# Expert weights as chunks of 2 k-tiles by 1024 columns, gate then linear then down, with 1024-column activation and bias rows padded to 128

## The chip, the cores and the metric

The kernel runs on one core of a Trainium2 chip. The metric is the device time of one execution in microseconds, taken as the median of several runs. The engines are named as in the profile: PE (TensorE; PEld is its weight load), DVE (VectorE), ACT (ScalarE), POOL (GpSimd) and SP (SyncE, which here only issues transfers).

## The reference

The kernel computes one layer of a diffusion backbone on 512 tokens of width 1024: a windowed attention, a pooling mixer and an output projection, then 32 experts of which each token takes 4. Of this the change touches the experts:

```python
# each token: softmax over its 4 best of 32 router logits; expert e on its tokens:
gu = h2 @ w_gu[e] + b_gu[e]                 # (tokens, 2048): gate half, linear half
g = minimum(gu[:, :1024], 7.0)
l = clip(gu[:, 1024:], -7.0, 7.0)
a = (l + 1) * g * sigmoid(1.702 * g)
y = a @ w_down[e] + b_down[e]               # (tokens, 1024)
...
out = rmsnorm(x + gate2 * sum over the 4 experts of weight * y, final_g)
```

Inputs, weights and the output are float32.

## The kernel before, in words

The front part (to about 640 us) computes the attention, the mixer, the router and the tables that say which tokens go to which expert; the change leaves it alone but for two small constants. Then 32 experts follow, each with room for 96 tokens (CAP). A loop for overfull experts stands behind; it runs zero times on this input.

**Precision by splitting.** A float32 weight is used as a sum of two parts of a shorter format (F32R): `hi`, the cast, and `lo`, what the cast left over. The same is done with the tokens (`xT`, gate and linear input, transposed) and the activations (`aT`, input of the down projection). A product is three matmuls: hi x hi, lo x hi, hi x lo (activation part first).

**Chunks.** All expert weights, 32 x 12 MB, come as 384 chunks of 1 MB. A chunk is 4 k-tiles (4 x 128 rows of the weight matrix) by 512 columns, a tile of 128 x 4 x 512 and so 2 KB a row piece. Step c of the main loop does, in this order in the program: the cast of chunk c+3 on ACT (`mwh`, L1508), the operations due at this step, the subtraction of chunk c+3 on DVE (`mwl`, L1514), the load of chunk c+11 into a raw slot (`mw`, queue of SP, L1188), the remaining operations due, then the 12 matmuls of chunk c (L1250, from `mm_chunk`), of 96 x 128 by 128 x 512 each. There are 8 raw slots (RS; a different order R0 for the first seven loads), 4 hi slots (HS) and 4 lo slots (LS).

**The order of chunks.** `GU` and `DN` give it. For each expert: gate, first 512 columns (two chunks, j=0); the second half of the preceding expert's down projection; linear j=0, gate j=1, linear j=1; the first half of its own down projection. At the second chunk of each of the four pieces a bias matmul follows (L1313): `selm` picks the expert's row, `bgh` holds 32 hi rows and 32 lo rows of all biases, so it runs on 64 rows. There are 128 of them.

**Work due at fixed steps.** A table `due`, filled by `at(step, function)`, places the rest between the chunks: `f_gm` (min), `f_sgm` (sigmoid, ACT), `f_gs` (product), `f_av` (clip, then product), each on 96 x 512 and twice per expert; `f_aT` and `f_x` (4 transposes on PE, hi and lo out of PSUM on ACT and DVE, L125), `f_y` (two halves, the down result times the token's weight, DVE) with the scatter that adds y to the result rows `acc` in memory (POOL, L1254), `f_gather` (token rows for an expert two on, POOL, tile `xgb`), and for experts 2 to 9 a share of the context bias (`abps`, tables). Names beginning with `f_ab`, `f_c`, `f_s`, `f_l` belong to these.

**The tail.** The last expert's result does not go through memory: it is put out by matmuls with a one-hot table (`fin`, L1388) and added (L1389) to `fx`, the rows of `acc` loaded back after the scatter of expert 30 (L1377); a final norm and the output follow. In the tail the lo of chunk 381 is on POOL (`PLO`) and the last lo's are ordered by hand (`los`).

Of the kernel before, what the change touches and what calls it, by code (L numbers as in the profile page):

```python
# [19 lines left out]
P = 128  # L20
# [48 lines left out]
def body(ctx, tc, x, c, cx, c_ctx, w_ada, b_ada, norm1_g, norm2_g, w_in, b_in, attn_sink, w_pool,  # L69
# [1109 lines left out]
    RS, HS, LS = (9, "wa1", 4, 10, 5, 6, 3, 2), (7, 0, 1, 18), (14, 19, 16, 13)  # L1179
    R0 = (9, 10, 4, 5, 6, 3, 2)  # L1180
    mr = {"r": 0, "h": 0, "x": 0}

    def mload(src):
        r = mr["r"]
        i = R0[r] if r < len(R0) else RS[(r - len(R0)) % len(RS)]
        raw = wa([P, 4, L], F32, "mw", 1) if i == "wa1" else slot(i, [P, 4, L], F32, "mw")
        mr["r"] += 1
        nc.sync.dma_start(raw, src)  # L1188
        return raw

    def msplit(raw):
        hi = slot(HS[mr["h"] % len(HS)], [P, 4, L], F32R, "mwh")
        lo = slot(LS[mr["h"] % len(LS)], [P, 4, L], F32R, "mwl")
        mr["h"] += 1
# [47 lines left out]
    def new_aT(j):  # L1242
        return slot(("17a", "17b")[j], [P, 2, 4, CAP], F32R, f"aT{j}")
# [54 lines left out]
    def bg_load():  # L1298
        bg["r"] = slot(18, [2 * NE, 2 * D], F32, "bgr")
        for i in range(2):  # L1300
            nc.sync.dma_start(bg["r"][i * NE:(i + 1) * NE, :], b_gu)

    def bg_hi():
        bg["h"] = slot(15, [2 * NE, 2 * D], F32R, "bgh")
        act.copy(bg["h"], bg["r"])
# [11 lines left out]
    def chunk_mm(st, kind, j, kh, w):  # L1317
        if kind == "d":
            if kh == 0 and j == 0:
                st["dn"] = [ps_b(("PV", "PJ")[q], "dn")[0:CAP] for q in range(2)]  # L1320
            mm_chunk(st["dn"][j], lambda a, kk: st["aT"][kh][:, a, kk - 4 * kh, :], kh, w, kh == 0, kh == 1)
            return
        if kh == 0:
            st[kind] = ps_s("gu")[0:CAP, 0:L]
        mm_chunk(st[kind], lambda a, kk: st["xT"][:, a, kk, :], kh, w, kh == 0, False)
        if kh == 1:
            st["bias"](st[kind], (D if kind == "l" else 0) + j * L)
# [12 lines left out]
    def f_av(st):  # L1340
        ln = wb([P, L], F32, "ln")[0:CAP]
        dve.tensor_scalar(ln, st["l"], LIMIT, -LIMIT, op0=ALU.min, op1=ALU.max)
        st["av"] = wk.tile([P, L], F32, tag="tv", bufs=1, name="av")[0:CAP]
        dve.scalar_tensor_tensor(st["av"], ln, 1.0, st["gm"], op0=ALU.add, op1=ALU.mult)

    def f_aT(st, j):
        if j == 0:
            st["aT"] = [None, None]
        st["aT"][j] = new_aT(j)
        trans_split(st["av"], st["aT"][j][:, 0], st["aT"][j][:, 1])  # L1350
# [16 lines left out]
    def fin_load():  # L1367
        fin["y"] = slot(3, [P, 2, D], F32R, "yhl")
        fin["g"] = slot(2, [P, D], F32, "fgr")
        nc.sync.dma_start(fin["g"], bc_row(final_g, D))  # L1370
        fin["j"] = slot(7, [P, D], F32, "fjk")
        fin["x"] = [slot((4, 10, 5, 6)[t], [P, 2, D], F32, "fx") for t in range(NT)]
        fx_load()
# [123 lines left out]

    def do_load(c):
        if c < len(chunks):
            raws[c] = mload(chunk_src(*chunks[c]))  # L1500

    def do_hi(c):
        if c < len(chunks):
            raw = raws.pop(c)
            hi = slot(HS[mr["h"] % len(HS)], [P, 4, L], F32R, "mwh")
            lo = slot(LS[mr["h"] % len(LS)], [P, 4, L], F32R, "mwl")
            mr["h"] += 1
            act.copy(hi, raw)  # L1508
# [15 lines left out]
    base = 0  # L1524
    for e in range(NE):
        st, n = ST[e], base
        w = 2 if e else 0
        pos = lambda s_: n + s_ - (0 if s_ < 2 else 2 - w)
        nx = pos(12)
        at(pos(2 if e else 4), f_gm, st), at(pos(2 if e else 4), f_sgm, st), at(pos(3 if e else 5), f_gs, st)  # L1530
        last = e == NE - 1
        at(pos(6), f_av, st)
        if not last:
            at(pos(8), f_aT, st, 0)
        at(pos(8), f_gm, st), at(pos(8), f_sgm, st), at(pos(9), f_gs, st)
        if last:
            at(pos(8), f_aT, st, 0)
        at(pos(10), f_av, st)
        at(pos(11) if last else nx, f_aT, st, 1)
        at(nx + (1 if last else 3), f_y, st, 0), at(nx + (2 if last else 4), f_y, st, 1)  # L1540
        if not last:
            at(pos(10), f_x, ST[e + 1], 0), at(pos(11), f_x, ST[e + 1], 1)
# [197 lines left out]
```

## Time and profile before

| | before |
|---|---|
| median of 3 runs | 1895.07 us (1890.53 to 1896.86) |
| profiled execution, its own time | 1895.16 us |
| its span | 1893.3 us |
| mean granted clock | 0.971 |
| PE busy in the span | 1767.9 us (93%), 8318 matmuls |
| DVE busy | 1627.4 us (86%) |
| ACT busy | 1138.3 us (60%) |
| POOL busy | 498.8 us (26%) |

The span is the profiled execution from its first to its last instruction; 1.9 us of its time lie outside. Busy shares are averages over a front part of 640 us and the experts behind it, which have other limits, and so say little by themselves; the rows further down are taken from stretches of the experts' part. A granted clock of 1.00 is 2.4 GHz.

### The profile page before, as it was taken

The numbers are of one execution on the slowest core, as the hardware profiler recorded it, in microseconds if no ns is written. First come the engines' busy times: TensorE is split into PE (matmuls) and PEld (weight loads), VectorE is DVE, ScalarE is ACT, GpSimd is POOL, SyncE is SP. The second block draws the span as 40 slices with busy tenths as digits, with TensorE's granted clock in tenths as the row PEclk, the third lists the DMA queues.
The fourth block names the chain that finished last, engine by engine and source line by source line (L and its number), as shares of the span: only waits on it lengthen the run. The fifth ranks groups of instructions, "written<-read, shape, count | busy, mean of one in ns | idle before, by whom it ended". The sixth has DMA issues, their size and how long they took to land.

```text
span 1893.3 us, 22494 instructions
## 1 busy us (share of the span) xinstructions
PE 1767.9 (93%) x8318; PEld 1257.9 (66%) x8318; DVE 1627.4 (86%) x1791; ACT 1138.3 (60%) x1221; POOL 498.8 (26%) x288
## 2 busy tenths in 40 slices
PE   4987989999999599999999999999999999999995
PEld 2676767877679466656666666666666666666663
DVE  6479998848875689888999999999999999999995
ACT  3255657763242266656676666667667676766763
POOL 5035544322441301212121112211311221131111
PEclk8799999999999799999999999999999999999997
DMA  9032322234555589999999999999999999999983
GB/s 323 1 112 67 126 88 88 78 129 146 196 189 202 183 296 356 332 320 339 353 355 338 357 362 352 350 359 363 350 355 361 352 354 357 359 352 351 362 313 108
DMA packets 278987, 508.06 MB, mean 268 GB/s; under 512 B 12561, under 2 KB 69022, under 8 KB 278810
## 3 DMA queue, kind: packets, MB, share of 16 engines
q1 hardware_dynamic: 271242, 487.97, 73.6%
q0 software_dynamic: 7632, 18.61, 4.2%
q8 instruction: 67, 1.10, 0.2%
q14 instruction: 46, 0.38, 0.1%
HBM read 490.02 MB, written 24.79 MB: 272 GB/s over the span
## 4 chain that ended last, share of the span: by engine, by line
PE 64%; DVE 4%; DMA 1%; issue 0%; POOL 0%; ACT 0%; SPq 0%; DVEq 0%; POOLq 0%; ACTq 0%
PE gu L1250 37%; PE dn L1250 18%; PE trps L1232 3%; PE gu L1313 3%; PE ops L131 2%; DVE mwl L1514 1%; DMA xgb<-h2d,igs 1%; DMA fx<-acc 0%; PE lgps L1092 0%; DVE xh L1071 0%; DVE xh L1057 0%; PE abps L1276 0%; DVE fx L1389 0%; PE h2ps L1085 0%; DVE fx L1402 0%
## 5 line engine op out<-in xcount | busy, mean ns | idle before, releaser
L1508 ACT CAST mwh<-mw 128x2048 fp32r<-128x2048 f32 x384 | 733.1, 1911 | 346.1 <-PE gu L1250 226.0
L1514 DVE TENSOR_TENSOR mwl<-mw,mwh 128x2048 fp32r<-128x2048 f32 x381 | 867.9, 2283 | 61.9 <-ACT mwh L1508 61.7
L1250 PE MATMUL gu<-mwh,xT 128*96 128x512 f32 x2048 | 647.7, 397 | 0.0
L1250 PEld LDWEIGHTS gu<-mwh,xT 128*96 128x96 f32 x2048 | 322.7, 162 | 143.8 <-issue 14.1
L1250 PE MATMUL gu<-mwl,xT 128*96 128x512 f32 x1024 | 404.9, 395 | 0.0
L1254 POOL DMA_INDIRECT acc<-y,igs x31 | 151.1, 4874 | 875.9 <-DVE y L1356 875.9
L1250 PE MATMUL dn<-mwh,aT 128*96 128x512 f32 x1024 | 325.9, 399 | 0.0
L1250 PEld LDWEIGHTS gu<-mwl,xT 128*96 128x96 f32 x1024 | 165.0, 161 | 72.1
L1250 PEld LDWEIGHTS dn<-mwh,aT 128*96 128x96 f32 x1024 | 158.1, 162 | 66.6 <-issue 7.8
L1250 PE MATMUL dn<-mwl,aT 128*96 128x512 f32 x512 | 202.1, 395 | 0.0
L704 PE MATMUL fps<-hx,whi 128*128 128x512 f32 x352 | 122.7, 407 | 1.8 <-ACT rope_t L588 0.8
L1250 PEld LDWEIGHTS dn<-mwl,aT 128*96 128x96 f32 x512 | 82.5, 161 | 36.1
L1211 POOL DMA_INDIRECT xgb<-h2d,igs x32 | 81.1, 2534 | 22.1 <-PE trps L1232 7.8
L704 PEld LDWEIGHTS fps<-hx,whi 128*128 128x128 f32 x352 | 66.8, 191 | 18.0 <-ACT gzt L577 2.3
L704 PE MATMUL fps<-hx,wlo 128*128 128x512 f32 x176 | 70.8, 402 | 2.0 <-POOL wlo L689 2.0
L508 ACT ACTIVATE prob<-S,nm 128x512 f32<-128x512 f32 (+1 forms) x64 | 47.8, 747 | 35.3 <-DVE nm L504 34.8
L1313 PE MATMUL gu<-bgh,selm 64*96 64x512 f32 x128 | 59.9, 468 | 0.0
L515 PE MATMUL tp<-ident,prob 128*128 128x128 f32 x288 | 45.5, 281 | 14.2 <-DVE pl L523 13.6
L1335 ACT ACTIVATE sgm<-gm 96x512 f32<-96x512 f32 x64 | 40.5, 633 | 28.5 <-DVE gm L1331 28.5
L523 DVE TENSOR_TENSOR pl<-tp,ph 128x512 fp32r<-128x512 f32 x72 | 49.2, 684 | 9.6 <-ACT ph L519 9.2
L503 DVE TENSOR_REDUCE nm<-S 128x1 f32<-128x512 f32 (+1 forms) x64 | 47.9, 749 | 6.3 <-PE S L478 6.1
L1313 PEld LDWEIGHTS gu<-bgh,selm 64*96 64x96 f32 x128 | 19.8, 155 | 50.2 <-issue 50.2
(388 smaller groups left out, 2627.1 us busy)
## 6 DMA issues: line engine op xcount, KB each, us to landing
mw<-in_w_gu_dram SPq DMA_DIRECT2D x256, 1024.0 KB
mw<-in_w_down_dram SPq DMA_DIRECT2D x128, 1024.0 KB
wada<-in_w_ada_dram SPq DMA_DIRECT2D x24, 1024.0 KB
gz<-gzt SPq DMA_DIRECT2D x16, 256.0 KB
sg<-gz SPq DMA_DIRECT2D x16, 256.0 KB
wo<-in_w_out_dram SPq DMA_DIRECT2D x4, 1024.0 KB
xt<-in_x_dram SPq DMA_DIRECT2D x2, 1024.0 KB
xh<-in_x_dram SPq DMA_DIRECT2D x4, 512.0 KB
```

Source lines behind the costliest of these rows:

```text
L503: dve.reduce_max(nmh, S[:, 0:W], axis=AX.X)
L508: act.activation(U["prob"][:, h, 0:W], S[:, 0:W], AF.Exp, bias=nmh, scale=SCALE, accum_out=U["den"][:, h:h + 1])
L515: pe.transpose(U["tp", j][:, h * P:(h + 1) * P], U["prob"][:, h, j * P:(j + 1) * P], ident)
L523: dve.tensor_sub(pl, U["tp", j], U["ph", j].bitcast(F32))
L704: pe.matmul(pt, a[:, k, :], b(k), start=n == 0, stop=n == 3 * KT - 1)
L1211: pool.indirect_dma_start(out=xg, out_offset=None, in_=h2d, in_offset=bass.IndirectOffsetOnAxis(ap=ig, axis=0), bounds_check=L - 1, oob_is ...
L1232: pe.transpose(pt[:, k * CAP:(k + 1) * CAP], src[:, k * P:(k + 1) * P], ident[0:CAP, 0:CAP])
L1250: pe.matmul(o, lhs(a, kk), b[:, k, :], start=first and k == 0 and a == 0 and b is wh, stop=last and k == 3 and b is wl)
L1254: pool.indirect_dma_start(out=acc, out_offset=bass.IndirectOffsetOnAxis(ap=iscat, axis=0), in_=y, in_offset=None, bounds_check=L - 1, oob_ ...
L1313: pe.matmul(o, selm[:, e:e + 1].to_broadcast([2 * NE, CAP]), bg["h"][:, c0:c0 + L], start=False, stop=True)
L1508: act.copy(hi, raw)
L1514: eng.tensor_sub(lo, raw, hi.bitcast(F32))
```

## The change

A chunk becomes 2 k-tiles by 1024 columns (128 x 2 x 1024, a row piece of 4 KB, still 1 MB). An expert's order becomes four gate chunks, four linear chunks, four down chunks of the preceding expert. The 12 matmuls of a chunk take hi x hi, lo x hi, hi x lo for both k-tiles, and in each the two column halves one behind the other, into two PSUM banks, with one stationary operand. The activation runs once per expert on 96 x 1024, in a tile `gs` that takes the fourth lo slot (13), so three lo slots are left; the subtraction of chunk c+3 and the load of chunk c+11 move behind the matmuls of chunk c. The bias tile gets 64 rows of zeros, so that its matmuls run on 128 rows. The dues are placed anew, with both halves of y at one step; in the tail POOL's subtraction and the orders by hand go, `fin_load` (final gain, slots) and `fx_load` (the rows of `acc`) become two steps, and the slots are taken from the ring.

```diff
-    RS, HS, LS = (9, "wa1", 4, 10, 5, 6, 3, 2), (7, 0, 1, 18), (14, 19, 16, 13)
-    R0 = (9, 10, 4, 5, 6, 3, 2)
+    RS, HS, LS = (9, 10, 4, 5, 6, 3, 2, "wa1"), (7, 0, 1, 18), (14, 19, 16)
...
-    selm = cp.tile([2 * NE, NE], F32R, name="selm")
-    dve.tensor_add(selm, ident[0:2 * NE, 0:NE], ident[0:2 * NE, NE:2 * NE])
+    selm = cp.tile([P, NE], F32R, name="selm")
+    dve.tensor_add(selm, ident[:, 0:NE], ident[:, NE:2 * NE])
...
-    def mm_chunk(o, lhs, kh, w, first, last):
+    def mm_chunk(os_, lhs, w, first, last, by_half=False):
         wh, wl = w
-        for k in range(4):
-            kk = 4 * kh + k
-            for a, b in ((0, wh), (1, wh), (0, wl)):
-                pe.matmul(o, lhs(a, kk), b[:, k, :], start=first and k == 0 and a == 0 and b is wh,
-                          stop=last and k == 3 and b is wl)
+        seq = [(k, a, b, j) for a, b in ((0, wh), (1, wh), (0, wl)) for k in range(2) for j in range(2)]
+        if by_half:
+            seq = sorted(seq, key=lambda x: x[3])
+        seen, left = set(), [x[3] for x in seq]
+        for k, a, b, j in seq:
+            left.remove(j)
+            pe.matmul(os_[j], lhs(a, k), b[:, k, j * L:(j + 1) * L], start=first and j not in seen,
+                      stop=last and j not in left)
+            seen.add(j)
...
     def bg_load():
-        bg["r"] = slot(18, [2 * NE, 2 * D], F32, "bgr")
+        bg["r"] = slot(18, [P, 2 * D], F32, "bgr")
+        pool.memset(bg["r"][2 * NE:], 0.0)
...
-            pe.matmul(o, selm[:, e:e + 1].to_broadcast([2 * NE, CAP]), bg["h"][:, c0:c0 + L], start=False,
+            pe.matmul(o, selm[:, e:e + 1].to_broadcast([P, CAP]), bg["h"][:, c0:c0 + L], start=False,
...
     def f_av(st):
-        ln = wb([P, L], F32, "ln")[0:CAP]
-        dve.tensor_scalar(ln, st["l"], LIMIT, -LIMIT, op0=ALU.min, op1=ALU.max)
-        st["av"] = wk.tile([P, L], F32, tag="tv", bufs=1, name="av")[0:CAP]
-        dve.scalar_tensor_tensor(st["av"], ln, 1.0, st["gm"], op0=ALU.add, op1=ALU.mult)
+        dve.tensor_scalar(st["sl"], st["l"], LIMIT, -LIMIT, op0=ALU.min, op1=ALU.max)
+        dve.scalar_tensor_tensor(st["gm"], st["sl"], 1.0, st["gm"], op0=ALU.add, op1=ALU.mult)
...
+    for e in range(NE):
+        chunks += [(e, kind, kk) for kind in "gl" for kk in range(4)]
+        if e:
+            chunks += [(e - 1, "d", kk) for kk in range(4)]
+    chunks += [(NE - 1, "d", kk) for kk in range(4)]
...
+        at(g + 4, f_gm, st), at(g + 4, f_sgm, st), at(g + 5, f_gs, st)
+        at(l + 4, f_av, st)
+        t0 = idx[e + 1, "g", 0] if e + 1 < NE else l + 4
+        at(t0 + 1, f_aT, st, 0), at(t0 + 2, f_aT, st, 1)
+        at(d + 4, f_y, st, 0), at(d + 4, f_y, st, 1)
...
+    at(nch - 6, fin_oh), at(nch - 5, fin_load), at(nch - 2, fx_load)
...
-        for c in range(nc_ + 1):
+        for c in range(nch + 1):
             do_hi(c + LS_)
...
+            for fn, a in due.pop(c, []):
+                fn(*a)
+            if c < nch:
+                e, kind, kk = chunks[c]
+                chunk_mm(ST[e], kind, kk, spl.pop(c))
+            do_lo(c + LS_)
+            do_load(c + LS_ + len(RS))
```

Three places show how the order on an engine moves. A wait in brackets names the semaphore that the instruction waits for: DMAHW those of loads from SP's queue, DMASW those of gathers and scatters, PE_49, Activation_49, Pool_49 and DVE_49 those of engines.

**DVE in the steady part.** From an expert's first activation to the next, before:

```order
L1342 TENSOR_SCALAR ln<-gu 96x512 [waits PE_49]
L1344 SCALAR_TENSOR_TENSOR av<-ln,gm 96x512 [waits DVE_49]
L1514 TENSOR_TENSOR mwl<-mw,mwh 128x2048 [waits DMAHW4_49,PE_49,Activation_49]
L1331 TENSOR_SCALAR gm<-gu 96x512 [waits PE_49]
L1514 TENSOR_TENSOR mwl<-mw,mwh 128x2048 [waits DMAHW5_49,Activation_49]
L125 TENSOR_TENSOR aT_9431<-trps,aT_9431 128x384 [waits Activation_49]
L1514 TENSOR_TENSOR mwl<-mw,mwh 128x2048 [waits DMAHW6_49,PE_49,Activation_49]
L1338 TENSOR_TENSOR gm<-gm,sgm 96x512 [waits DVE_49]
L1514 TENSOR_TENSOR mwl<-mw,mwh 128x2048 [waits DMAHW7_49,PE_49,Activation_49]
```

and of the change, where `gs` is the tile of 1024 columns that takes the place of gm, sgm, ln and av:

```order
L1522 TENSOR_TENSOR mwl<-mw,mwh 128x2048 [waits DVE_49,DMAHW7_49,PE_49,Activation_49]
L1345 TENSOR_TENSOR gs<-gs 96x1024 [waits Activation_49]
L1522 TENSOR_TENSOR mwl<-mw,mwh 128x2048 [waits DMAHW0_49,PE_49,Activation_49]
L1522 TENSOR_TENSOR mwl<-mw,mwh 128x2048 [waits DMAHW1_49,PE_49,Activation_49]
L1522 TENSOR_TENSOR mwl<-mw,mwh 128x2048 [waits DVE_49,DMAHW2_49,PE_49,Activation_49]
L1348 TENSOR_SCALAR gs<-gu 96x1024 [waits DVE_49,PE_49]
L1349 SCALAR_TENSOR_TENSOR gs<-gs 96x1024 [waits DVE_49]
L1522 TENSOR_TENSOR mwl<-mw,mwh 128x2048 [waits DMAHW3_49,PE_49,Activation_49]
L125 TENSOR_TENSOR xT<-trps,xT 128x384 [waits Activation_49]
L1522 TENSOR_TENSOR mwl<-mw,mwh 128x2048 [waits DMAHW4_49,PE_49]
```

The activation operations are half as many and twice as wide, two of them still one behind the other, and every subtraction now waits for PE.

**DVE at the end.** The last subtractions, `y` and the first `fx` addition (`ohT` is the one-hot table, `yhl` hi and lo of the last y), before:

```order
L1514 TENSOR_TENSOR mwl<-mw,mwh 128x2048 [waits DMAHW3_49]
L1424 TENSOR_SCALAR ohT<-iota_14892,ltok 96x512 [waits Pool_49]
L1356 SCALAR_TENSOR_TENSOR y<-dn,gts,g2r 96x512 [waits DMASW0_49,PE_49]
L1381 TENSOR_TENSOR yhl<-y,yhl 96x512 [waits DMAHW1_49,Activation_49]
L1356 SCALAR_TENSOR_TENSOR y<-dn,gts,g2r 96x512 [waits PE_49]
L1389 TENSOR_TENSOR fx<-fx,fin 128x512 [waits DMAHW5_49,PE_49]
```

and of the change:

```order
L1435 TENSOR_SCALAR ohT<-iota_14378,ltok 96x512 [waits Pool_49]
L1522 TENSOR_TENSOR mwl<-mw,mwh 128x2048 [waits DMAHW1_49,PE_49]
L1522 TENSOR_TENSOR mwl<-mw,mwh 128x2048 [waits DVE_49,DMAHW2_49,PE_49,Activation_49]
L1365 SCALAR_TENSOR_TENSOR y<-dn,gts,g2r 96x512 [waits DMASW7_49]
L1365 SCALAR_TENSOR_TENSOR y<-dn,gts,g2r 96x512
L1522 TENSOR_TENSOR mwl<-mw,mwh 128x2048 [waits DVE_49,DMAHW3_49,PE_49,Activation_49]
L1365 SCALAR_TENSOR_TENSOR y<-dn,gts,g2r 96x512 [waits DMASW1_49,PE_49]
L1392 TENSOR_TENSOR yhl<-y,yhl 96x512 [waits Activation_49]
L1365 SCALAR_TENSOR_TENSOR y<-dn,gts,g2r 96x512 [waits PE_49]
L1400 TENSOR_TENSOR fx<-fx,fin 128x512 [waits DMAHW5_49,PE_49]
```

Expert 30's two y operations, which end in the scatter that `fx_load` waits for, now stand just ahead of the very last subtraction.

**SP's queue at the first experts.** The loads around the last write of `acc`, before:

```order
L1188 DMA mw<-in_w_gu_dram 128x4x512 [waits DMAHW0_49,Pool_49]
L1188 DMA mw<-in_w_down_dram 128x4x512 [waits DMAHW1_49]
L1188 DMA mw<-in_w_down_dram 128x4x512 [waits DMAHW2_49,DVE_49]
L1078 DMA acc<-xh 128x1024 [waits DMAHW3_49]
L1188 DMA mw<-in_w_gu_dram 128x4x512 [waits DMAHW4_49,Pool_49]
```

and of the change:

```order
L1186 DMA mw<-in_w_gu_dram 128x2x1024 [waits DMAHW0_49]
L1186 DMA mw<-in_w_gu_dram 128x2x1024 [waits DMAHW1_49,Pool_49]
L1186 DMA mw<-in_w_gu_dram 128x2x1024 [waits DMAHW2_49,Pool_49]
L1078 DMA acc<-xh 128x1024 [waits DMAHW3_49]
L1186 DMA mw<-in_w_gu_dram 128x2x1024 [waits DMAHW4_49,DVE_49]
```

The load ahead of the write of `acc` waits for POOL instead of DVE, the one behind it for DVE instead of POOL.

## Rows read from the trace of the kernel before

**Rows 1.** Windows: length, busy us (instructions) per engine, granted clock, DMA share, GB/s.

```profile
1750.00:1775.00 25.00, 25.00 (x109) 16.75 (x107) 23.52 (x19) 16.88 (x12) 5.44 (x1) 1.00 1.03 374
1020.00:1820.00 800.00, 800.00 (x3552) 536.43 (x3551) 755.58 (x565) 556.13 (x390) 174.89 (x43) 1.00 1.02 355
1460.00:1470.00 10.00, 10.00 (x43) 6.68 (x42) 8.56 (x7) 7.33 (x5) 0.00 (x0) 1.00 1.04 388
```

**Rows 2.** Waits, 1020 to 1820 us: us in total, times, longest.

```profile
DVE mwl L1514 <- ACT mwh L1508: 42.9, 67, 1.1
PEld gu L1313 <- issue: 34.1, 87, 0.4
```

**Rows 3.** Timeline of PE around a bias: start, us, what.

```profile
1854.72 0.63 PE L1250 MATMUL gu<-mwh,xT 128*96 128x512 f32 x2
1855.18 0.39 PE L1250 MATMUL gu<-mwl,xT 128*96 128x512 f32 x1
1855.50 0.47 PE L1313 MATMUL gu<-bgh,selm 64*96 64x512 f32 x1
1855.90 0.70 PE L1250 MATMUL dn<-mwh,aT 128*96 128x512 f32 x2
```

**Rows 4.** Timeline of PE ahead of matmuls of 32 and of 96 rows.

```profile
751.02 0.40 PE L1250 MATMUL gu<-mwl,xT 128*96 128x512 f32 x1
751.35 1.12 PE L1276 MATMUL abps<-bdn,gT 32*128 32x512 f32 x2
...
1858.53 0.39 PE L1250 MATMUL dn<-mwl,aT 128*96 128x512 f32 x1
1858.76 0.49 PE L1232 MATMUL trps<-ident,av 96*128 96x96 f32 x4
```

**Rows 5.** Timeline of PE in the tail.

```profile
1867.44 2.25 PE L1388 MATMUL fin<-yhl,ohT 96*128 96x512 f32 x9
```

**Rows 6.** Lines by shape, DVE, 1020 to 1820 us: busy, mean ns, idle before.

```profile
L1514 DVE TENSOR_TENSOR mwl<-mw,mwh 128x2048 fp32r<-128x2048 f32 x260 | 592.1, 2284 | 42.9 <-ACT mwh L1508 42.9
L1356 DVE SCALAR_TENSOR_TENSOR y<-dn,gts,g2r 96x512 f32<-96x512 f32 x44 | 32.6, 741 | 0.0
L1331 DVE TENSOR_SCALAR gm<-gu 96x512 f32<-96x512 f32 x44 | 29.9, 680 | 0.0
```

**Rows 7.** Lines by shape, DVE 1870 to 1893 and POOL 520 to 640 us.

```profile
L1402 DVE SCALAR_TENSOR_TENSOR fx<-fx,rs,fgr 128x1024 f32<-128x1024 f32 x3 | 3.7, 1281 | 0.0
...
L1202 POOL MEMSET xgb<- 96x1024 f32 x2 | 1.8, 948 | 2.8 <-PE brps L131 2.8
```

**Rows 8.** Waits, 720 to 1020 us.

```profile
DVE y L1282 <- DMA acc<-y,igs: 12.0, 4, 3.2
...
PE trps L1232 <- DVE xT L125: 2.9, 5, 0.7
...
PE trps L1232 <- DVE aT L125: 1.5, 4, 0.6
```

**Rows 9.** The chain that ended last: start, us, what.

```profile
654.81 10.36 DMA xgb<-h2d,igs
...
1861.53 7.86 DMA fx<-acc
```

**Rows 10.** Tile views: scatters (acc, whole run), then gathers (xgb, 640 to 700).

```profile
DMA to landing us min/median/max: 7.1/12.3/13.3
...
DMA to landing us min/median/max: 4.0/8.7/10.4
```

**Rows 11.** Timelines: POOL and SP in the head, SP and DVE in the tail.

```profile
636.54 4.66 POOL L1514 TENSOR_TENSOR mwl<-mw,mwh 128x2048 fp32r<-128x2048 f32 x1 [1.80 <-ACT mwh L1508]
643.90 13.39 SPq L1188 DMA_DIRECT2D mw<-in_w_down_dram  x2
...
1860.15 1.93 SPq L1377 DMA_DIRECT2D fx<-acc  x4
...
1870.11 3.67 DVE L1389 TENSOR_TENSOR fx<-fx,fin 128x512 f32<-128x512 f32 x6
```

More of the change, by code (lines that the diff above doesn't have):

```diff
@@ L1303, in bg_hi @@
     def bg_hi():
-        bg["h"] = slot(15, [2 * NE, 2 * D], F32R, "bgh")
+        bg["h"] = slot(15, [P, 2 * D], F32R, "bgh")
         act.copy(bg["h"], bg["r"])
@@ L1322, in chunk_mm @@
             return
[L1323 to L1327, printed above, removed]
+        if first:
+            st[kind] = ps_s("gu")[0:CAP, :]
+        halves_ = [st[kind][:, j * L:(j + 1) * L] for j in range(2)]
+        mm_chunk(halves_, lambda a, k: st["xT"][:, a, 2 * kk + k, :], w, first, False)
+        if last:
+            for j in range(2):
+                st["bias"](halves_[j], (D if kind == "l" else 0) + j * L)
@@ L1347, in f_aT @@
         if j == 0:
-            st["aT"] = [None, None]
-        st["aT"][j] = new_aT(j)
-        trans_split(st["av"], st["aT"][j][:, 0], st["aT"][j][:, 1])
+            if st is ST[-1]:
+                both = wa([P, 2, 2, 4, CAP], F32R, "aTe", 0)
+                st["aT"] = [both[:, 0], both[:, 1]]
+            else:
+                st["aT"] = [slot(i, [P, 2, 4, CAP], F32R, "aT") for i in ("17a", "17b")]
+        t = st["aT"][j]
+        trans_split(st["gm"][:, j * L:(j + 1) * L], t[:, 0], t[:, 1])
@@ L1367, in fin_load @@
     def fin_load():
-        fin["y"] = slot(3, [P, 2, D], F32R, "yhl")
-        fin["g"] = slot(2, [P, D], F32, "fgr")
+        s_ = [RS[i % len(RS)] for i in range(nch - len(RS), nch)]
+        fin["free"] = s_[6:]
+        fin["y"] = slot(s_[5], [P, 2, D], F32R, "yhl")
+        gj = slot(s_[3], [P, 2, D], F32, "fgj")
+        fin["g"], fin["j"] = gj[:, 0], gj[:, 1]
         nc.sync.dma_start(fin["g"], bc_row(final_g, D))
-        fin["j"] = slot(7, [P, D], F32, "fjk")
-        fin["x"] = [slot((4, 10, 5, 6)[t], [P, 2, D], F32, "fx") for t in range(NT)]
-        fx_load()
+        fin["x"] = [wa([P, 2, D], F32, "fx", 1) if i == "wa1" else slot(i, [P, 2, D], F32, "fx")
+                    for i in (s_[0], s_[1], s_[2], s_[4])]
     def fx_load():
@@ L1496, in body @@
+    chunks += [(NE - 1, "d", kk) for kk in range(4)]
+    idx = {c: i for i, c in enumerate(chunks)}
+    nch = len(chunks)
     raws, spl = {}, {}
     def do_load(c):
-        if c < len(chunks):
+        if c < nch:
             raws[c] = mload(chunk_src(*chunks[c]))
     def do_hi(c):
-        if c < len(chunks):
+        if c < nch:
             raw = raws.pop(c)
-            hi = slot(HS[mr["h"] % len(HS)], [P, 4, L], F32R, "mwh")
-            lo = slot(LS[mr["h"] % len(LS)], [P, 4, L], F32R, "mwl")
-            mr["h"] += 1
+            hi = hi_tile()
@@ L1525, in body @@
     for e in range(NE):
[L1526 to L1542, printed above, removed]
+        st = ST[e]
+        g, l, d = (idx[e, kind, 0] for kind in "gld")
+        at(g + 4, f_gm, st), at(g + 4, f_sgm, st), at(g + 5, f_gs, st)
+        at(l + 4, f_av, st)
+        t0 = idx[e + 1, "g", 0] if e + 1 < NE else l + 4
```

131 lines of the change are left out of this document (54 added, 77 removed).

## The prediction

> **What bounds the kernel now.** I read the granted clock first, then busy time by stage, then the waits of the stage that fills most of the span, then its head and tail. From 1020 to 1820 us the matmul engine (PE) is busy for 800.00 of 800 us at granted clock 1.00, which is 2.4 GHz, while DVE has 755.58 and ACT 556.13 [rows 1]. Nothing that the other engines or the DMA queues do ends any wait of PE there: the list of waits names none for its matmuls, and for its weight loads before a bias only "issue", 0.4 us, 87 times [rows 2]. So in this stage time is the sum of PE's steps. 87 bias matmuls at four to an expert are 21.75 experts in 800 us, 36.8 us each. DVE is the next: its lo subtractions wait for the hi cast for 42.9 us in all [rows 2], so it is busy 755.58/21.75 = 34.7 us of each 36.8.
>
> **PE's steps.** A step is the time from the start of one matmul to the next. Two plain ones go from 1854.72 to 1855.18, 0.23 us each; the last plain one of a chunk and the bias behind it go from 1855.18 to 1855.90, 0.72 us for two [rows 3]. The bias costs 0.72 - 0.46 = 0.26 us more than a step of its 512 columns. It differs from its neighbours by 64 rows against 128. Before the 32-row matmuls the step is long too, 751.02 to 751.35; before transposes with 96 rows it is not, 1858.53 to 1858.76 [rows 4]. I take it that the change of row count is what costs, and that 128 rows take it away: **128 biases x 0.26 = -33.3 us**. The opposite bound is nothing (the second rival).
>
> The rest of PE's work is as many matmuls of the same size. New is that two in a row share a stationary operand and write to two banks. The nearest row is the end of the kernel, where pairs share one: nine steps in 2.25 us, so (2.25 - 0.39)/8 = 0.23 each [rows 5], no gain and no loss. The transposes are as many as before. So an expert takes 36.8 - 4 x 0.26 = 35.8 us.
>
> **Can DVE follow?** Eight operations of 0.68 us on 512 columns [rows 6] become four on 1024; the nearest row for that width is 1.28 us [rows 7]. That is 5.44 - 5.12 = 0.3 us less, so 34.4 of the 35.8 us: DVE stays below PE if it never idles over 1.4 us an expert. The new wait is that with three lo buffers lo(c+3) needs the buffer of chunk c, so it stands behind chunk c's matmuls (12 x 0.23 = 2.77 us a chunk) and everything queued behind it on DVE stands too: the activation operations, the xT and aT splits, y. PE first reads this lo at the ninth matmul of chunk c+3, 32 steps or 7.4 us after the buffer is free; the subtraction takes 592.1/260 = 2.28 us [rows 6]. The worst pile is at the first down chunk: one lo, the two av operations (2.56), the next lo, less the 2.77 us that a chunk gives, is 2.28 + 2.56 + 2.28 - 2.77 = 4.36, which leaves 3 us. In the experts with context biases y waits up to 3.2 us for a scatter (12.0 us in four waits) [rows 8], and there the margin is just used up. I take the wait as hidden: **0**, and keep the price for the case that it is not (third rival). If DVE does come late, PE is late next, and the loads are not: 8 slots are 8 x 2.77 = 22 us.
>
> **Experts 2 to 9.** From 720 to 1020 us PE waits 2.9 us for xT splits and 1.5 us for aT splits on DVE [rows 8]. These come where a lo and an activation stand ahead of a split that the next chunk needs. In the new order xT is split one and two chunks into the down part, and first needed two chunks later; aT in the next expert's gate part, six chunks before it is needed. **-3 us**, between -4.4 and 0.
>
> **The transfers.** A row of a chunk grows from 2 to 4 KB, with the same bytes. They must come at 355 x 36.8/35.8 = 365 GB/s instead of 355 [rows 1]. Stretches of before run at 374 and 388 GB/s, PE still full [rows 1]; so I cost it at **0**. The Trainium skill, "DMA: Bandwidth & Descriptors", section "Specifications", gives about 358 GB/s as the limit of HBM for one core and elsewhere on the page says that it binds here. By that figure an expert takes 355/358 x 36.8 = 36.5 us, and the sum would be near 1889. The two stretches disagree with it, though they are short and could be slots refilled after a pause. A cap by the rows alone is the first rival.
>
> **The head.** The chain goes through the first gather, 10.36 us from 654.81 to landing [rows 9]; the other gathers there land in 4.0 to 8.7 us [rows 10]. At its side go a weight load and the write of acc that the SP queue released at 656.9 (643.90 + 13.39 less its 0.4 us issue) and a further load [rows 11], which stood behind a slot that DVE frees. In the new ring that slot is freed by POOL, which frees it earlier, so one load of 1 MB goes ahead of the gather instead of beside it: **-1.7 us** (10.4 to the median 8.7), from -6.4 to 0. The memset of 64 rows by 2048 on POOL is about twice a 96 by 1024 one of 0.95 us [rows 7]; POOL idles 1.80 us ahead of its first lo [rows 11], so 0, or up to +1.9 if it stands on the path.
>
> **The tail.** Before, the scatter of expert 30's y is issued while 8 chunks are still to come; now y(30) is at the step of the fourth last chunk, on DVE behind lo of the second last, which may start when the fifth last chunk ends. From there: 2.28 for the lo, 2 x 0.74 for y, 0.7 of backlog from the one-hot operation two steps earlier (one operation on 512 columns) [rows 6], 7.1 us to landing (the last scatter, alone, is taken for the minimum; the median is 12.3) [rows 10]: 11.6 us, against 4 x 2.77 = 11.1 to the end E of the weights' matmuls (1867.44 before [rows 5]). The loads of fx read what that scatter writes, so they start at E + 0.5. Before they were out at 1860.15 [rows 11] and took until 1861.53 + 7.86 = 1869.39 [rows 9], 9.2 us with the final gain's row ahead of them in the queue; now that row is gone earlier, four fifths are 7.4 us. Five of the six adds behind them (3.67 us for six [rows 11]) are 3.1 us. The last add ends at E + 0.5 + (7.4 to 9.2) + 3.1 = E + 11.0 to 12.8, against 1870.11 + 3.67 - 1867.44 = E + 6.3 before: **+5.5 us**, between 4.7 and, with a scatter of 13.3 us, 11.7. From there to the end nothing changes.
>
> **The sum** against the profiled execution's own 1895.16 us (0.1 above the median of the runs shown): 1895.16 - 33.3 - 3 - 1.7 + 5.5 = 1862.7, said as **1862 us**. All favourable ends give 1895.16 - 33.3 - 4.4 - 6.4 + 4.7 = 1856, the unfavourable 1895.16 - 33.3 + 0 + 1.9 + 11.7 = 1875.5.
>
> **The rivals.**
> 1. The transfers cap it: the queue gives no more than the 355 GB/s of the long window, raw slots run empty, ACT's cast waits for DMA, and an expert takes 36.8 us as before. That is 1895.16 - 1.7 + 5.5 = 1899 us, or 1896 with the 3 us of experts 2 to 9, no change. For it: the DMA share is 1.02 already [rows 1]. Against: 374 and 388 GB/s over stretches, and no wait of ACT for a load among the waits of 800 us. 0.05.
> 2. The 0.26 us is not the rows' but that of the broadcast stationary operand, or of the turn to another source; it stays. 1895.16 - 3 - 1.7 + 5.5 = 1896 us, no change. Against: the 32-row matmuls have the same long step with an ordinary operand [rows 4]. 0.04.
> 3. **Slower: the hand-over of the lo buffers stops DVE.** Each lo now waits for PE's last matmul on its buffer, and the engine is in order. It decides from (35.8 - 34.4)/12 = 0.12 us of idle DVE time per lo on; against the old pace of 36.8, from 0.2. The waits for ACT in the trace are 42.9/67 = 0.64 us when they occur [rows 2]. If half the lo's had such a wait, DVE needs 34.4 + 6 x 0.64 = 38.2 us an expert, 1.4 more than now: 32 x 1.4 = 45, with -1.7 + 5.5, so about 1944 us. For it: one buffer less, and DVE at 94%. Against: the 7.4 us between buffer free and first use; a DVE that waits for PE is by that ahead, not late. 0.07.
> 4. The second weight load of a pair is skipped and PE runs nearer to 512 columns at 2.4 GHz, 0.213 us: 2304 of the 4608 steps gain 0.019 each, 43 us, which gives 1862 - 43 = 1819 us. The row of pairs at the end shows no such gain [rows 5]. 0.04.
>
> **How the numbers follow.** A measurement of this kernel can tell about 0.3% (5.7 us) from no change. The main case has 0.80 and lies in 1856 to 1876. The range, 1852 to 1880, takes that in, a few us below for steps a nanosecond shorter (4608 x 1 ns = 4.6 us), and above for a DVE that is late in experts 2 to 5 only. Faster: main and the fourth, 0.84. Same: the first two, 0.09, which lie within 0.3% of before. Slower: 0.07.
>
> **What would show it.** Right: in the steady stage PE stays full, the step from the last plain matmul over the bias is twice 0.23, biases come 87 x 36.8/35.8 = 89 to 90 times in 800 us, and DVE's idle time stands on "PE", not PE's on DVE. The tail shows a wait of SP for the scatter of y, and fx landing some 8 to 10 us after E. Wrong: waits of PE for mwl (third rival), of ACT for mw from DMA (first), the lead of 0.32 us still there (second), plain steps under 0.225 (fourth).

## The result and the profile after

The changed kernel takes 1865.04 us (median of 4 runs, 1857.19 to 1867.19) against 1894.84: ratio 0.9838, 95% interval 0.9805 to 0.9871. The profiled execution takes 1864.69 us, with a span of 1862.9. The first section of its page, and windows of the steady stage (length, busy us per engine, granted clock, DMA share, GB/s) and of the last matmuls:

```profile
PE 1729.9 (93%) x8318; PEld 1272.3 (68%) x8318; DVE 1613.8 (87%) x1664; ACT 1122.2 (60%) x1189; POOL 452.9 (24%) x288
```

```profile
1020.00:1790.00 770.00, 770.00 (x3555) 543.45 (x3554) 748.09 (x478) 545.43 (x370) 109.61 (x43) 1.00 1.00 369
1820.00:1824.00 4.00, 0.81 (x3) 0.23 (x1) 3.59 (x3) 1.33 (x1) 0.00 (x0) 0.92 0.00 0
1824.00:1828.00 4.00, 4.00 (x13) 2.68 (x13) 0.02 (x1) 0.00 (x0) 1.43 (x1) 0.65 0.42 52
```

In the steady stage PE is full as before [rows 1]. An expert is 164 matmuls and transposes, so it takes 770 x 164/3555 = 35.5 us, where the same count of before gives 800 x 164/3552 = 36.9. DMA moves 369 GB/s where it moved 355, and no engine waits for a load. The bias now stands in the row of its neighbours (timeline of PE, answering to [rows 3]):

```profile
1805.37 0.85 PE L1254 MATMUL gu<-mwl,xT 128*96 128x512 f32 x3
1806.06 0.63 PE L1316 MATMUL gu<-bgh,selm 128*96 128x512 f32 x2
1806.53 0.62 PE L1254 MATMUL dn<-mwh,aT 128*96 128x512 f32 x2
```

Two biases take 1806.53 - 1806.06 = 0.47 us, twice a plain step. DVE (waits from 1020 to 1790 us, and the lines of the new activation) waits for PE and no longer for the cast [rows 2], as an engine does that is ahead; an operation on 1024 columns takes 1.22 us where I took 1.28:

```profile
DVE mwl L1522 <- PE gu L1254: 20.7, 43, 0.5
```

```profile
L1348 DVE TENSOR_SCALAR gs<-gu 96x1024 f32<-96x1024 f32 x22 | 26.7, 1214 | 0.0
```

Three places went another way. First, experts 2 to 9 (waits, 720 to 1020 us, answering to [rows 8], and from the timeline of POOL the issue of one of the scatters that DVE waits for there):

```profile
DVE y L1287 <- DMA acc<-y,igs: 16.4, 4, 5.7
...
PE trps L1236 <- DVE aT L125: 7.2, 5, 2.6
```

```profile
773.30 5.93 POOL L1259 DMA_INDIRECT acc<-y,igs  x1 [12.26 <-DVE y L1365]
```

Second, the first expert (timeline of PE). The gather still lands late, and PE then stops once more for the second expert's xT, at a place where before it had down chunks:

```profile
661.59 1.54 PE L1236 MATMUL trps<-ident,xgb 96*128 96x96 f32 x8 [10.42 <-DMA xgb<-h2d,igs]
...
692.75 1.37 PE L1254 MATMUL gu<-mwh,xT 128*96 128x512 f32 x4 [2.68 <-DVE xT L125]
```

Third, the tail (timelines of PE, of DVE and POOL, of SP):

```profile
1811.14 0.52 PE L1236 MATMUL trps<-ident,gs 96*128 96x96 f32 x4 [1.68 <-DVE gs L1349]
...
1823.51 3.65 PE L1254 MATMUL dn<-mwh,aTe 128*96 128x512 f32 x8 [3.19 <-DVE y L1365]
...
1827.92 2.01 PE L1254 MATMUL dn<-mwh,aTe 128*96 128x512 f32 x8
...
1836.59 0.50 PE L1399 MATMUL fin<-yhl,ohT 96*128 96x512 f32 x1
```

```profile
1820.41 2.29 DVE L1522 TENSOR_TENSOR mwl<-mw,mwh 128x2048 fp32r<-128x2048 f32 x1 [0.55 <-PE dn L1254]
1822.62 1.40 DVE L1365 SCALAR_TENSOR_TENSOR y<-dn,gts,g2r 96x512 f32<-96x512 f32 x2
...
1839.65 3.67 DVE L1400 TENSOR_TENSOR fx<-fx,fin 128x512 f32<-128x512 f32 x6
```

```profile
1829.50 1.77 SPq L1388 DMA_DIRECT2D fx<-acc  x4
```

PE stands 3.19 us for y of expert 30, and its next eight matmuls take 3.65 us instead of 2.01, at a granted clock of 0.65: down of expert 31 writes the two PSUM banks that y(30) still has to read, and y(30) stands behind a lo. In the steady part eight chunks lie between; at the end none. Some 10 us earlier the transposes of the last activation wait 1.68 us; in the kernel before they had no wait [rows 4].

### The profile page after: what moved, and what is told of

It is laid out like the page before. It is cut to its first block, busy times and chain, and to the rows that moved or that the text cites. A ratio compares the mean times of both kernels' runs of the same rounds, so it can differ in the third digit from the quotient of the medians.

```text
span 1862.9 us, 22522 instructions
## 1 busy us (share of the span) xinstructions
PE 1729.9 (93%) x8318; PEld 1272.3 (68%) x8318; DVE 1613.8 (87%) x1664; ACT 1122.2 (60%) x1189; POOL 452.9 (24%) x288
## 5 line engine op out<-in xcount | busy, mean ns | idle before, releaser
L1254 PE MATMUL gu<-mwh,xT 128*96 128x512 f32 x2048 | 522.4, 397 | 3.0 <-DVE xT L125 2.7
L1259 POOL DMA_INDIRECT acc<-y,igs x31 | 117.6, 3793 | 860.8 <-DVE y L1365 860.8
L1254 PE MATMUL gu<-mwl,xT 128*96 128x512 f32 x1024 | 279.5, 395 | 0.0
L1254 PE MATMUL dn<-mwh,aT 128*96 128x512 f32 x992 | 252.8, 397 | 0.0
L1254 PE MATMUL dn<-mwl,aT 128*96 128x512 f32 x496 | 135.1, 394 | 0.4 <-DVE mwl L1522 0.4
L1342 ACT ACTIVATE gs<-gs 96x1024 f32<-96x1024 f32 x32 | 34.0, 1062 | 101.5 <-DVE gs L1339 101.5
L1215 POOL DMA_INDIRECT xgb<-h2d,igs x32 | 71.3, 2227 | 45.8 <-DMA mw<-in_w_gu_dram 24.5
L1365 DVE SCALAR_TENSOR_TENSOR y<-dn,gts,g2r 96x512 f32<-96x512 f32 x64 | 44.9, 740 | 4.6 <-PE dn L1254 4.6
L519 ACT CAST ph<-tp 128x512 fp32r<-128x512 f32 x72 | 41.9, 584 | 5.1 <-PE tp L515 4.6
```

Source lines behind the costliest of these rows:

```text
L519: act.copy(U["ph", j], U["tp", j])
L1215: pool.indirect_dma_start(out=xg, out_offset=None, in_=h2d, in_offset=bass.IndirectOffsetOnAxis(ap=ig, axis=0), bounds_check=L - 1, oob_is ...
L1254: pe.matmul(os_[j], lhs(a, k), b[:, k, j * L:(j + 1) * L], start=first and j not in seen, stop=last and j not in left)
L1259: pool.indirect_dma_start(out=acc, out_offset=bass.IndirectOffsetOnAxis(ap=iscat, axis=0), in_=y, in_offset=None, bounds_check=L - 1, oob_ ...
L1365: dve.scalar_tensor_tensor(st["y"][:, cs], st["dn"][n], st["gt"], g2r[0:CAP, cs], op0=ALU.mult, op1=ALU.mult)
```

## The experiments

All times are medians of 4 to 6 runs; kernels of one group shared the runs of before (medians 1893.2 to 1894.8). The runs of one kernel lie 3 to 13 us apart, those of the change 10, so a difference of a few us between two medians is not shown to be real.

**1. The padding alone, on the kernel before.**

```diff
-    selm = cp.tile([2 * NE, NE], F32R, name="selm")
+    selm = cp.tile([P, NE], F32R, name="selm")
...
+        pool.memset(bg["r"][2 * NE:], 0.0)
```

> The kernel before with nothing but the 64 zero rows added to the bias operands. Theory (the switch between 64 and 128 rows costs 0.26 us at each bias): 128 x 0.26 = 33.5 us less than before, about 1861 us, and the step from the last plain matmul to the bias falls from 0.326 to 0.23 us, the one behind it from 0.40 to 0.23. Rival (the gain comes from the new order of chunks, from the shared stationary operand or from the wide activation): no change, about 1895 us.

Measured: 1859.98 us, ratio 0.9818 (0.9800 to 0.9835). The padding alone carries all of the gain; by medians it gains 5 us more than the whole change, but the intervals of the two ratios overlap. Its window of the steady stage and the timeline of PE at a bias:

```profile
1020.00:1780.00 760.00, 760.00 (x3499) 535.71 (x3498) 741.33 (x557) 546.43 (x383) 230.89 (x43) 1.00 1.04 368
```

```profile
1820.02 0.39 PE L1250 MATMUL gu<-mwl,xT 128*96 128x512 f32 x1
1820.25 0.39 PE L1314 MATMUL gu<-bgh,selm 128*96 128x512 f32 x1
1820.48 0.62 PE L1250 MATMUL dn<-mwh,aT 128*96 128x512 f32 x2
```

760 x 164/3499 = 35.6 us an expert, 1.3 less than before: 0.33 us for each of its four biases, not 0.26. In experts 2 to 9 PE waits longer than before for aT and xT (4.6 and 3.8 us against 1.5 and 2.9 [rows 8]), so 32 x 1.3 = 42 us did not all arrive.

**2. The change with 64 bias rows.**

```diff
-    selm = cp.tile([P, NE], F32R, name="selm")
+    selm = cp.tile([2 * NE, NE], F32R, name="selm")
...
-        pool.memset(bg["r"][2 * NE:], 0.0)
```

> The changed kernel with the bias operands back at 64 rows, all else as changed. Theory: the gain of the padding goes, 1865 + 33.5 = 1898 us, a few us slower than before. Only one of two biases that follow each other is next to a plain matmul on each side, so if the cost is paid per switch and not per bias, half of it comes back: 1865 + 17 = 1882 us. Rival (order and layout carry the gain): about 1865 us.

Measured: 1880.18 us, ratio 0.9926 (0.9902 to 0.9951). Timeline of PE at a pair of biases:

```profile
1821.70 0.85 PE L1254 MATMUL gu<-mwl,xT 128*96 128x512 f32 x3
1822.48 0.70 PE L1315 MATMUL gu<-bgh,selm 64*96 64x512 f32 x2
1823.11 0.93 PE L1254 MATMUL dn<-mwh,aT 128*96 128x512 f32 x3
```

The three steps around a pair are 0.31 to 0.32 us each, together 0.25 us more than three plain ones: as much for two biases as the two steps of one were before (0.26). So the cost is paid per switch and not per bias: 15 us are lost again, not 33. (Its steady stage alone, 3439 steps in 760 us, loses 0.7 us an expert, 22 us. Against that, PE waits 0.9 us for aT in experts 2 to 9 in this profile; run 3 shows how that wait varies.)

**3. The change with 96 bias rows.**

```diff
-        bg["r"] = slot(18, [P, 2 * D], F32, "bgr")
+        bg["r"] = slot(18, [3 * NE, 2 * D], F32, "bgr")
```

> The changed kernel with the bias operands at 96 rows (32 of zeros). If any row count other than that of the neighbours costs a switch, the time is that of the run with 64 rows. If 96 rows run as 128 do, as the transposes of 96 rows suggest, which follow plain matmuls after 0.23 us, it is that of the change, 1865 us.

Measured: 1866.04 us, ratio 0.9848 (0.9830 to 0.9867), that of the change; two biases take 0.47 us (timeline of PE):

```profile
1800.53 0.63 PE L1316 MATMUL gu<-bgh,selm 96*96 96x512 f32 x2
1801.00 0.63 PE L1254 MATMUL dn<-mwh,aT 128*96 128x512 f32 x2
```

So a differing row count is not what costs; 96 rows run as 128 do, 64 do not. The Trainium skill, "TensorEngine Tiling (Array Packing)", section "Key Properties", says that a change of tiling mode drains the engine; runs 1 to 3 fit that if 64 rows set another mode and 96 rows do not, but no trace shows the mode.

Run 3 also shows how much experts 2 to 9 differ from one execution to the next. Its code there is the change's, and so is the order on DVE. Its profile is of an execution of 1859.20 us (waits from 720 to 1020 us, and the timeline of POOL):

```profile
DVE y L1287 <- DMA acc<-y,igs: 8.9, 4, 2.7
...
PE trps L1236 <- DVE aT L125: 1.5, 4, 0.7
```

```profile
774.40 3.26 POOL L1259 DMA_INDIRECT acc<-y,igs  x1 [12.26 <-DVE y L1365]
```

In that stretch four scatter issues of the change's profile take 5.9 us and one 11.1; here one takes 10.8 and the others 3.2 to 3.4. DVE waits 16.4 us for scatters there and 8.9 here, and PE waits 7.2 us for aT there and 1.5 here.

**4. No shared stationary operand.**

```diff
-        if by_half:
-            seq = sorted(seq, key=lambda x: x[3])
+        seq = sorted(seq, key=lambda x: x[3])
```

> The changed kernel with the 12 matmuls of every chunk sorted by column half, so that no two in a row share a stationary operand or turn to another bank; the lo part is now first read at the fifth of the 12 instead of the ninth. If the shared operand is what makes a plain step 1.4 ns shorter than before (0.2329 against 0.2369 us with the lead to the bias left in), 4608 x 1.4 ns = 6 us are lost, 1871 us. If sharing does nothing, 1865 us. If DVE has no spare time left, PE waits for the lo and it is slower by more than 10 us.

Measured: 1874.75 us, ratio 0.9885 (0.9864 to 0.9906). In 760 us it makes 3479 steps where the change makes 3507: 35.8 against 35.5 us an expert, 9 us over 32 or about 2 ns a step, and PE waits for nothing there. The edit takes away the shared operand and the turn between two banks together, and run 1, which has neither, needs only 35.6 us an expert; so the 9 us are not shown to be the shared operand's. It does not skip the second load: that would be 19 ns a step, and the change's window counts 3554 loads on 3555 matmuls.

**5. Another PSUM buffer for the last down result.**

```diff
+                if st is ST[-1]:
+                    dn = ps_s("dnl")[0:CAP, :]
+                    st["dn"] = [dn[:, q * L:(q + 1) * L] for q in range(2)]
```

> The changed kernel with the down result of the last expert in a PSUM buffer of the gate and linear results instead of the two banks that y of expert 30 still reads. Theory (at the end of the fifth last chunk PE waits for y because both down results use the same two banks; in the steady part eight chunks lie between): the wait of 3.35 us and the low clock behind it (0.65 over 4 us) go, so the weights end about 5 us earlier. But the loads of fx, which wait for the scatter of that y, then end behind the matmuls and give 2 to 3 us back: about 2.5 us faster than the change, 1862 us. If fx is no limit: 1860 us. Rival (PE waits there for the lo of the last chunks): unchanged, 1865 us.

Measured: 1865.01 us, ratio 0.9851 (0.9833 to 0.9869). The stall is gone, the time is not less. Timelines of PE, POOL, SP and DVE:

```profile
1820.60 2.02 PE L1254 MATMUL dnl<-mwh,aTe 128*96 128x512 f32 x8
```

```profile
1824.75 3.23 POOL L1259 DMA_INDIRECT acc<-y,igs  x1 [33.62 <-DVE y L1369]
```

```profile
1831.89 1.77 SPq L1392 DMA_DIRECT2D fx<-acc  x4
```

```profile
1839.95 3.08 DVE L1404 TENSOR_TENSOR fx<-fx,fin 128x512 f32<-128x512 f32 x5 [0.56 <-DMA fx<-acc]
```

The scatter lands 7.1 us after its issue, fx is loaded from then, and its last adds wait for it: the tail that I had priced.

**6. The same, with y(30) ahead of a lo, and the last transposes one step later.**

```diff
+            if c == nch - 5:
+                f_y(ST[-2], 0), f_y(ST[-2], 1)
```

> As the run before, and besides y of expert 30 stands ahead of the lo of the second last chunk on DVE instead of behind it, and the transposes of the last activation come one step later. Theory: the scatter starts 2.3 us earlier, so what fx gives back is gone, and the wait of 1.8 us for the last activation's transposes is gone too: about 7 us faster than the change, 1858 us. If the scatter is not what fx waits for: no better than the run before.

Measured: 1865.27 us, ratio 0.9851 (0.9837 to 0.9864), not the 7 us. PE has no wait left before the last chunk, and y is some 4 us earlier in its tail than in the run before, but the scatter's issue on POOL grows (timelines of POOL and DVE):

```profile
1818.74 5.43 POOL L1259 DMA_INDIRECT acc<-y,igs  x1 [29.84 <-DVE y L1369]
```

```profile
1818.37 4.49 DVE L1526 TENSOR_TENSOR mwl<-mw,mwh 128x2048 fp32r<-128x2048 f32 x2
```

Where DVE is idle the same issue takes 1.43 us, behind one lo 3.23, behind two in a row 5.43: it ends some 1.3 us after the lo. From the last bias to the last add this profile takes 35.0 us, that of run 5 36.3 and that of the change 37.0, so 2 of the 7 us are there, less than the medians can show.

**7. The context work two steps later, and xT ahead of the last activation operations in expert 0.**

```diff
-            at(g + 1, f_abm, e - 2, 0), at(g + 3, f_abv, e - 2, 0)
+            at(g + 3, f_abm, e - 2, 0), at(g + 5, f_abv, e - 2, 0)
```

> The changed kernel with the context bias of experts 2 to 5 and the counting of experts 8 and 9 two steps later (its matmul after both transposes of the preceding activation, the DVE operation two steps behind), and the second expert's xT split ahead of the first expert's last two activation operations on DVE. Theory (the context's PSUM buffer, held from the first to the third gate chunk, leaves one buffer for the two transposes of an activation, so the second waits for DVE's split of the first): the waits of PE for aT, 7.2 us, and for xT in the first expert, 2.7 us, go, with a slow-clock stretch behind the longest: 8 to 10 us faster, about 1856 us. Rival (DVE is late there whatever the order, since it waits 16.4 us for scatters): 0 to 3 us, 1863 us.

Measured: 1856.85 us, ratio 0.9806 (0.9793 to 0.9820), as expected. PE has one wait left from 720 to 1020 us:

```profile
PE lstps L1469 <- DVE nbb L1465: 1.6, 1, 1.6
```

The wait for aT is gone, but DVE's waits for scatters are gone there too. So this run does not tell the held buffer from a DVE that is late because of the scatters, and part of the 7.2 us can be the execution's own (run 3). Its five runs, 1855.99 to 1860.24 us, do lie lower and closer than the change's.

**8. Two lo buffers.**

```diff
-    RS, HS, LS = (9, 10, 4, 5, 6, 3, 2, "wa1"), (7, 0, 1, 18), (14, 19, 16)
+    RS, HS, LS = (9, 10, 4, 5, 6, 3, 2, "wa1"), (7, 0, 1, 18), (14, 19)
...
-        do_lo(2)
...
-            do_lo(c + LS_)
+            do_lo(c + LS_ - 1)
```

> The changed kernel with two lo buffers instead of three, so that each lo may begin one chunk (2.77 us) later, 20 steps or 4.7 us before PE reads it. The pile worked out at the first down chunk, 4.36 us, still fits by 0.3 us. If the slack was as worked out: the steady part loses less than 0.3 us an expert, 0 to 10 us in all, 1865 to 1875 us. If the hand-over already used it up with three buffers: 2.8 us at every expert and more, over 1940 us. If DVE were far ahead: unchanged.

Measured: 1851.34 us, ratio 0.9780 (0.9766 to 0.9793): **14 us faster**, which no theory had. The steady stage is the same (3506 steps in 760 us against 3507), so DVE is ahead even so. The gain is at the head, where the lo of chunk 2 had moved behind the first xT, and in the context part, where the waits for aT are 1.0 us and not 7.2 (1.5 in run 3, without this edit). Run 9 takes the first of these alone.

**9. Only the lo of chunk 2 behind the first xT.**

```diff
-        do_lo(2)
         gates_g(2)
...
             f_x(ST[0], i)
+        do_lo(2)
```

> The changed kernel with one thing moved: the lo of chunk 2 stands behind the first expert's xT splits on DVE, not ahead of them. Theory (in the run with two lo buffers PE's first matmul came 4.4 us after the gather's issue instead of 10 because no lo ran on DVE beside that issue, 1.24 against 3.20 us on POOL, and because no slot was freed for a weight load that goes beside the gather): 5 to 6 us faster than the change, 1859.5 us, the gather landing in some 4.5 us. If only the issue on POOL counts: 2 us, 1863 us. Rival (that run was faster by its two buffers and the later lo, not by the head): unchanged, 1865 us.

Measured: 1852.89 us, ratio 0.9789 (0.9769 to 0.9809). Timelines of POOL and SP of this run, and the wait of PE:

```profile
651.63 1.24 POOL L1215 DMA_INDIRECT xgb<-h2d,igs  x1 [5.25 <-DVE igs L1165]
```

```profile
661.04 16.90 SPq L1186 DMA_DIRECT2D mw<-in_w_gu_dram  x6
```

```profile
656.13 1.54 PE L1236 MATMUL trps<-ident,xgb 96*128 96x96 f32 x8 [5.03 <-DMA xgb<-h2d,igs]
```

and of the change:

```profile
651.70 3.20 POOL L1215 DMA_INDIRECT xgb<-h2d,igs  x1 [5.25 <-DVE ltok L1170]
```

```profile
653.82 28.16 SPq L1186 DMA_DIRECT2D mw<-in_w_gu_dram  x6
```

The issue is 2 us shorter, and the weight load that the lo's slot let go at 653.82 now comes at 661.04; the transposes begin 4.5 us after the gather's start instead of 9.9. That explains 5.4 of the 12 us. Most of the others lie between the second and the eleventh expert, from one's last bias to the other's: 333.6 us here and 341.6 in the change's profile, but 334.0 in that of run 3, whose code there is the change's. They go with the scatters (DVE waits 8.5 us for them here, 8.9 in run 3, 16.4 in the change's profile). Whether the edit has a part in that stays open.

**10. These together.** Two lo buffers, context and xT as in run 7 (the counting of expert 8 a step earlier), tail as in run 6.

```diff
-    RS, HS, LS = (9, 10, 4, 5, 6, 3, 2, "wa1"), (7, 0, 1, 18), (14, 19, 16)
+    RS, HS, LS = (9, 10, 4, 5, 6, 3, 2, "wa1"), (7, 0, 1, 18), (14, 19)
...
+        if e == 0:
+            at(l + 4, f_x, ST[1], 0), at(l + 4, f_x, ST[1], 1)
         at(l + 4, f_av, st)
```

> The version that the runs point to: the changed kernel with two lo buffers and each lo one chunk later, the context bias two steps later, the second expert's xT ahead of the first's last activation, and the tail of the run with another PSUM buffer and the earlier y. If the parts add up: 1851.3 less 2.5 for xT, 1 for the context and 2 for the tail, 1846 us. If the tail's scatter is still held up on POOL behind the lo's: 1848 us.

Measured: 1844.23 us, ratio 0.9749 (0.9732 to 0.9766), the fastest of the study. The tail edit brings nothing here; from the last bias to the last add it takes 37.0 us, as the change does:

```profile
1801.10 7.63 POOL L1259 DMA_INDIRECT acc<-y,igs  x1 [29.90 <-DVE y L1369]
```

**11. Runs 1 and 9 together, on the kernel before.**

```diff
+        pool.memset(bg["r"][2 * NE:], 0.0)
...
-        do_lo(2)
...
             f_x(ST[0], i)
+        do_lo(2)
```

> The kernel before with the 64 zero rows and with the lo of chunk 2 behind the first xT splits; order, chunk shape and activation as before. Theory (the head's gain does not depend on the new order): 1860 less 5 to 6, 1854.5 us. If the gain in the head belongs to the new ring of slots: 1860 us.

Measured: 1861.65 us, ratio 0.9827 (0.9813 to 0.9841): nothing, though the gather landed in 4.1 us. Timelines of ACT and PE:

```profile
663.76 5.51 ACT L1509 CAST mwh<-mw 128x2048 fp32r<-128x2048 f32 x3 [5.19 <-DVE bgh L1310]
```

```profile
670.76 0.70 PE L1250 MATMUL gu<-mwl,xT 128*96 128x512 f32 x1 [2.22 <-DVE mwl L1515]
```

The fourth cast needs the hi slot that holds the bias rows until DVE has made their lo, which now stands behind the lo of chunk 2. Most of the gain is given back soon after: from the first gate matmul to the first expert's last bias it takes 30.5 us here and 25.6 in run 1.

**12. Run 10 with the one-hot operation between the first and second lo after y(30).**

```diff
+            if c == nch - 5:
+                fin_oh()
```

> The version before it with the one-hot operation of DVE (one input from SBUF and a scalar, 0.47 us) set between the first and the second of the three lo subtractions that stand behind y of expert 30. Theory (the issue of a scatter or gather on POOL waits for the end of a lo that runs on DVE, and for the next too where none or only one operation of another kind lies between, which is what made it 7.63 us there): the issue ends after the first lo, 3.2 us, the rows of the scatter land 4.4 us earlier, and with them the loads of fx: up to 4 us faster, 1840 us. If the issue is long for another reason: 7.6 us and 1844 us as before it.

Measured: 1845.72 us, ratio 0.9755 (0.9741 to 0.9770). Timelines of POOL and DVE:

```profile
1801.21 8.03 POOL L1259 DMA_INDIRECT acc<-y,igs  x1 [29.51 <-DVE y L1369]
```

```profile
1800.85 2.28 DVE L1530 TENSOR_TENSOR mwl<-mw,mwh 128x2048 fp32r<-128x2048 f32 x1
1803.05 0.48 DVE L1443 TENSOR_SCALAR ohT<-iota,ltok 96x512 fp32r<-96x512 f32 x1
1803.45 4.48 DVE L1530 TENSOR_TENSOR mwl<-mw,mwh 128x2048 fp32r<-128x2048 f32 x2
```

My expectation failed: 0.48 us of that operation between two lo's do not let the issue through. A split of aT between two lo's, which reads PSUM, is no sure way either. The scatters of the steady part, with such a split behind the first lo, take 3.24 us, but with the same order on DVE the one shown of the change takes 5.93 us at 773.30 and that of run 3 takes 3.26. What lets an issue through stays open. The Trainium skill, "SBUF — State Buffer", section "Who interferes with whom", gives DVE and POOL one port pair that a tensor-scalar operation can take, as can a two-input one against an operation of POOL that reads SBUF, and infers that a two-input one does not hold up the making of descriptors. The first fits this run. The inference is not borne out for the issue as a whole, since the lo, a two-input subtraction, held it up by 2 us and more; but the issue also reads the row numbers `igs` from SBUF, and no run tells that part from the making of descriptors. That a PSUM reader in the gap would repair the tail was not tried.

## Why the prediction was right

The 1862 us came out at 1865, by the main step: PE's steps set the time and the switch of row count was what the bias cost (runs 1 to 3). That the sum came within 3 us is in part luck: the padding gave some 9 us more than its term, and waits that the sum did not have or had the wrong way (experts 2 to 9, the second expert's xT, the last activation's transposes) took about as much. Step by step:

- **The bias, -33.3 us: right, the term too small.** In the steady stage the padding saves 1.3 us an expert (run 1), 42 us over 32. I read the two steps around the bias and missed that the transposes and the first matmul behind it are slower too. Nor does every change of row count cost, as I put it: 96 rows do not (run 3). The second rival is out: the broadcast operand is still there in run 1.
- **Shared operand, nothing: nearly.** Run 4, without it, is 9 us slower. But run 1 has no shared operand either, and the new order gains hardly anything on it: 35.5 against 35.6 us. The fourth rival is out.
- **DVE hidden, 0: right in the steady stage**, with more room than I gave it: even two buffers do (run 8). The third rival is out.
- **The transfers, 0: right.** 369 GB/s over 770 us, no wait for a load; the first rival is out, and so is the 358 GB/s of the Trainium skill ("DMA: Bandwidth & Descriptors", section "Specifications") as a limit for this core alone. (The 1889 us reckoned with it leaves out the 3 us of experts 2 to 9; with them it is 1886.)
- **Experts 2 to 9, -3 us: wrong.** PE waits 7.2 us for aT. The context matmul holds one of two PSUM buffers for the transposes from the first gate chunk to the third, so the second transpose of aT needs DVE's split of the first. I read when aT is needed, not which buffer its transposes write to. How long PE then waits goes with how late DVE is, and DVE is late after its waits for scatters, which I had read (3.2 us at most) and taken as hidden: at most 5.7 us in the change's profile, with 7.2 for aT, but 2.7 in run 3's, with 1.5. Run 7, which moves the context, removes both waits, so the share of each stays open.
- **The head, -1.7 us: wrong in its cause.** A load did go ahead of the gather, but another, freed by the lo of chunk 2, still went beside it, and that lo held up the gather's issue (run 9). Landing hardly changed. The 3.6 us by which the first gate matmul comes earlier stood there already in the front part: POOL's table operation of 613.25 us starts at 609.92, in code that the change leaves alone. The second expert's xT, 2.7 us, I had not priced.
- **The tail, +5.5 us: the size nearly right, the cause another.** The stall on PSUM and the low clock behind it came first, and covered the wait for fx, so the last add ends only 0.4 us later against E than before. With the 1.68 us of the last activation's transposes that is 1.68 + 3.19 + (3.65 - 2.01) + 0.4 = 6.9 us. Run 5, without the stall, shows the tail as worked out, landing of 7.1 us included, and the same time.

So the rest of the change, all but the padding, brings no gain. By medians it loses 5 us (1865.0 against 1860.0), which the spread of the change's runs (1857.19 to 1867.19) does not show to be a loss, and the shares of its parts are known only as far as runs 5 to 10 go.

## What to carry to other kernels

When an engine is full, read its steps one by one and look for the pair that is out of line; here one odd matmul in 37 was worth 2% and a few rows of zeros removed it. For every step that is moved to the end, or past a point where another holds a buffer, ask which buffer it writes and who reads that last: cover that holds in the middle of a loop is gone in its first and last round. Removing one of two waits that lie over each other shows next to nothing, as the tail did twice. And before a wait of one profile is put down to the code, read the same stretch in another execution of the same code: here it was 7.2 us in one and 1.5 in the next.

## What was not expected of the hardware

The issue of an indirect transfer on POOL takes 1.24 to 1.43 us with no lo on DVE beside it, and up to 8.03 us in the tail beside a row of these subtractions, which read two tiles of SBUF; with the same order on DVE it took 3.26 us in one execution and 5.93 in another. And 64 rows cost a switch where 96 cost none (0.32 against 0.23 us a step).
